# A hybrid DeltaNet and dilated-attention block: decay inputs moved into an attention unit, chain steps grouped, stores spread

## The chip, the cores and the metric

The kernel runs on one core of one Trainium2 chip, and the metric is its device time in microseconds. The engines are written as the profile writes them: PE is TensorE's matmul, PEld its weight load, DVE is VectorE, ACT is ScalarE, POOL is GpSimd and SP is SyncE, which here issues nearly all DMAs from its queue (SPq). "Clock" means the TensorE clock that the profile says was granted, 1.00 being the upper level.

## What is computed

One encoder layer on 512 tokens of width 1024, all in float32. A combined projection of the normed input feeds two branches, whose results are gated, merged, projected and added to the input; a convolved feed-forward network follows.

```python
h = RMSNorm(x); proj = h @ w_in
qkv_a, z_a, a_in, b_in, q_b, k_b, v_b, gate_a, gate_b = split(proj)
# branch A: bidirectional gated DeltaNet, 8 heads of 64, chunks of 64 tokens
q_a, k_a, v_a = silu(conv3(qkv_a));  q_a, k_a = l2norm(q_a), l2norm(k_a)
g = -exp(a_log) * softplus(a_in + dt_bias); beta = sigmoid(b_in)     # per direction and head
tmat = inverse(I + strict_lower((k*beta) @ k.T * decay))             # per chunk and head
...  # eight chunk steps that carry a state, both directions, summed, normed, * silu(z_a)
# branch B: attention, 3 groups of 8 heads, windows (128,1) (512,4) (2048,16), combined by softmax weights
x = x + (sigmoid(gate_a) * (o_a @ w_dn_out) + sigmoid(gate_b) * (o_b @ w_attn_out)) @ w_o
x = x + (silu(gate) * up) @ w_ffn_down      # gate, up = conv3(RMSNorm(x) @ w_ffn_up)
```

The decay inputs a_in and b_in are 32 columns of the projection in all: two directions by eight heads for each of the two.

## The kernel before

**Products.** Every large product is made of three matmuls on split numbers: mm3 (L321) multiplies high by high, high by low and low by high part, so PE's lines L322, L323 and L324 come in equal numbers. A dense tile is 128 output columns by 512 tokens: 8 blocks of the contraction by 3 matmuls, 24 matmuls 512 wide, in one dense PSUM tile (`dps`, four of them, PD). Chains use a second pool of four PSUM tiles (`gps`, PG).

**Weights.** Stream (L52) brings the weights in, in the order of use. SP loads a block into one of three staging tiles (`wst`, L67), ACT copies the high part (`whi`, L81), and POOL or DVE subtracts to get the low part (`wlo`, L83). Six pairs of parts are kept, three blocks ahead of use. SP's one queue also takes the chains' own loads and stores in the order in which the program issues them.

**The order of dense work** is written out by hand in SEQ (L39): K (four tiles), AB (the decay inputs: 32 columns, as 24 matmuls of 32 rows by 512 tokens), Q0 to Q3, U0, V0 to V3, Z0, U1, and so on to U11, then the last gates, YA, YB and WO. K, Q and V are the DeltaNet inputs, channels on partitions. A unit U is one attention group by two heads: 384 columns (q, k and v) as 96 matmuls 384 wide, tokens on partitions, in four dense PSUM tiles, one for each 128 tokens; att_dense (L642) takes all four at its start. Z and G tiles are the gates. Up to YA, chains run between the dense matmuls; after it comes a dense tail (YA, YB, WO, the feed-forward network).

**Chains.** All other work is in Python generators, and Driver (L121) places their steps while the program is built. It keeps a modelled time; each dense matmul group adds its cost, and after it due (L173) runs each chain step whose time has come. A chain's yield says how much later its next step may stand: LATE (1.5) after work whose result a PE step takes, LOAD (5.0) after a DMA, TRIP (8.0) after a round trip. The times are the planner's own and set only the order of instructions on each engine; at run time each engine takes its instructions in that order and waits on semaphores. room and need hold a step until a slot (T2: four [128, 512] work tiles; PG; PD) is free by the model.

**The chains that matter here.** After K, the row norm (L363 to L379) runs in line with the program and makes `rstd`. qkv_tile (L445) takes a Q, K or V tile from PSUM on DVE (L429), does the three-tap convolution (L432 on ACT, L434 and L435 on DVE), and the SiLU (L458, L459). decays (L488) transposes the AB rows on PE, does softplus and sigmoid arithmetic in 64-wide DVE and ACT steps (L505 to L525), and takes cumulative sums on PE (L531). k_tokens transposes K (L577). chain (L952) then forms the 64 by 64 systems and solves them in halves: eight stores of 32x32x32 pieces of `cx` go to DRAM in `dl`, in runs of 128 bytes (L987); one load brings them back as `lt` (L989); 31 solve steps of two DVE instructions each (L994, L997) follow; then a store, ten scattered loads back (L1014, L1017), block products, eight DeltaNet steps and post (L1288), which transposes the outputs (L1305) and splits them (`oa`, L1315, L1319) for YA. att_softmax (L728) takes each unit through scores, exps (Exp on ACT, L770), turn (four transposes per head and block of the probabilities, L782), and values (L798).

```python
def due(self, ahead=0.3):                                   # L173
    while True:
        d = [c for c in self.chains if c[1] <= self.now + ahead]
        if not d:
            return
        self.step(min(d, key=lambda c: c[1]))
...
for f in range(2):                                          # L982
    for a in range(2):
        for b in range(2):
            ...
            nc.sync.dma_start(du(dl)[f, a, b], cx[P, f].rearrange("p s h t -> p (s h) t")[:, :, b * 32:b * 32 + 32])     # L987
yield LOAD
nc.sync.dma_start(lt, dl)                                   # L989
```

## Time and profile before

| | |
|---|---|
| time, median of 3 runs | 1046.26 us (1045.7 to 1050.86) |
| time of the profiled execution | 1045.01 us |
| its span | 1043.2 us |
| mean granted clock | 0.982 |
| PE busy | 1001.0 us (96%), 6653 matmuls |
| PEld busy | 838.3 us (80%) |
| DVE busy | 676.1 us (65%) |
| ACT busy | 433.3 us (42%) |
| POOL busy | 252.8 us (24%) |

The times of the table are of one execution, the profiled one; what the span leaves out of its time is 1.8 us around the first and last instruction. A busy share is an average over stages with different limits, so the stage table (the first group of rows) is read first: it gives each engine's busy time in a stretch and how many instructions that is. The timeline then gives single waits: a bracket behind a row holds the idle time of the engine just before it and what ended that. A stretch of half clock shows only in the windows view, in the column after the busy times.

### The profile page before, as it was taken

The numbers are of one execution on the slowest core, as the hardware profiler recorded it, in microseconds if no ns is written. First come the engines' busy times: TensorE is split into PE (matmuls) and PEld (weight loads), VectorE is DVE, ScalarE is ACT, GpSimd is POOL, SyncE is SP. The second block draws the span as 40 slices with busy tenths as digits, with TensorE's granted clock in tenths as the row PEclk, the third lists the DMA queues.
The fourth block names the chain that finished last, engine by engine and source line by source line (L and its number), as shares of the span: only waits on it lengthen the run. The fifth ranks groups of instructions, "written<-read, shape, count | busy, mean of one in ns | idle before, by whom it ended". The sixth has DMA issues, their size and how long they took to land.

```text
span 1043.2 us, 17128 instructions
## 1 busy us (share of the span) xinstructions
PE 1001.0 (96%) x6653; PEld 838.3 (80%) x6653; DVE 676.1 (65%) x1139; ACT 433.3 (42%) x857; POOL 252.8 (24%) x229
## 2 busy tenths in 40 slices
PE   8989989987999989999999999899999999999998
PEld 7769788875998978988887878688888888888886
DVE  7594957756798746566867575577775326777621
ACT  6246545646554535324455133344433214344310
POOL 5334366623443532534532001200000000000000
PEclk9999989989999989999999999999999999999999
DMA  6223233462222491322365545313223222222331
GB/s 203 88 65 92 67 118 126 106 187 75 94 86 81 147 192 48 105 82 71 103 225 159 158 137 171 129 64 101 83 99 121 82 100 81 100 82 101 112 111 41
DMA packets 80289, 114.62 MB, mean 110 GB/s; under 512 B 32624, under 2 KB 45264, under 8 KB 79824
## 3 DMA queue, kind: packets, MB, share of 16 engines
q1 hardware_dynamic: 77328, 108.29, 33.8%
q10 hardware_dynamic: 2880, 5.24, 1.4%
q8 instruction: 52, 0.85, 0.3%
q14 instruction: 29, 0.24, 0.1%
HBM read 101.04 MB, written 12.47 MB: 109 GB/s over the span
## 4 chain that ended last, share of the span: by engine, by line
PE 67%; DVE 14%; issue 6%; ACT 5%; DMA 4%; POOL 2%; SPq 2%; POOLq 0%; ACTq 0%; DVEq 0%
PE dps L322 20%; PE dps L323 20%; PE dps L324 20%; DMA wst<-in_wa 3%; POOL wlo L83 2%; PE gps L747 1%; PE gps L798 1%; DVE wlo L83 1%; ACT sb L770 1%; DVE tmp L994 1%; ACT whi L81 1%; DVE ass L261 1%; PE gps L782 1%; DVE cy L434 1%; DVE ass L260 1%
## 5 line engine op out<-in xcount | busy, mean ns | idle before, releaser
L83 POOL TENSOR_TENSOR wlo<-wst,whi 128x384 fp32r<-128x384 f32 (+1 forms) x152 | 184.6, 1226 | 284.4 <-ACT whi L81 264.4
L81 ACT ACTIVATE whi<-wst 128x384 fp32r<-128x384 f32 (+2 forms) x259 | 174.4, 691 | 142.6 <-PE dps L323 70.7
L322 PE MATMUL dps<-h2h,whi 128*128 128x512 f32 x352 | 139.2, 395 | 0.0
L324 PE MATMUL dps<-h2h,wlo 128*128 128x512 f32 x352 | 139.1, 395 | 0.0
L323 PE MATMUL dps<-h2l,whi 128*128 128x512 f32 x352 | 139.0, 395 | 0.0
L83 DVE TENSOR_TENSOR wlo<-wst,whi 128x1024 fp32r<-128x1024 f32 (+2 forms) x107 | 117.6, 1106 | 20.9 <-ACT whi L81 20.8
L432 ACT ACTIVATE cy<-pre,vec 128x512 f32<-128x512 f32 x56 | 40.5, 724 | 142.1 <-DVE pre L429 142.0
L322 PE MATMUL dps<-whi,hr 128*128 128x384 f32 x256 | 92.3, 360 | 1.2 <-DVE v L672 0.6
L323 PE MATMUL dps<-wlo,hr 128*128 128x384 f32 x256 | 86.9, 339 | 0.0
L324 PE MATMUL dps<-whi,lr 128*128 128x384 f32 x256 | 86.9, 339 | 0.0
L323 PEld LDWEIGHTS dps<-h2l,whi 128*128 128x128 f32 x352 | 66.1, 188 | 16.0
L324 PEld LDWEIGHTS dps<-h2h,wlo 128*128 128x128 f32 x352 | 66.1, 188 | 16.0
L322 PEld LDWEIGHTS dps<-h2h,whi 128*128 128x128 f32 x352 | 66.1, 188 | 16.0
L434 DVE SCALAR_TENSOR_TENSOR cy<-pre,vec,cy 128x511 f32<-128x511 f32 x56 | 46.4, 828 | 36.3 <-ACT cy L432 36.3
L322 PE MATMUL dps<-ah,whi 128*128 128x512 f32 x176 | 69.8, 397 | 0.0
L323 PE MATMUL dps<-al__7594,whi 128*128 128x512 f32 x176 | 69.6, 396 | 0.0
L324 PE MATMUL dps<-ah,wlo 128*128 128x512 f32 x176 | 69.2, 393 | 0.0
L1430 DVE TENSOR_TENSOR x<-x,dps 128x512 f32<-128x512 f32 x16 | 11.0, 688 | 78.8 <-PE dps L324 78.8
L322 PE MATMUL dps<-hh,whi 128*128 128x512 f32 x128 | 53.4, 417 | 2.2 <-ACT hh L286 2.2
L770 ACT ACTIVATE sb<-sb,stat 128x128 f32<-128x128 f32 (+1 forms) x96 | 40.8, 426 | 33.9 <-DVE stat L759 33.8
L322 PE MATMUL dps<-hr,whi 128*128 128x512 f32 x120 | 50.0, 416 | 4.4 <-ACT v L677 4.4
L322 PE MATMUL dps<-whi,hh 128*128 128x384 f32 x128 | 46.7, 365 | 7.7 <-DVE z L1214 5.1
(298 smaller groups left out, 2116.2 us busy)
## 6 DMA issues: line engine op xcount, KB each, us to landing
wst<-in_wb SPq DMA_DIRECT2D x66, 512.0 KB, 3.2
wst<-in_wa SPq DMA_DIRECT2D x96, 256.0 KB, 2.7
wst<-in_wa SPq DMA_DIRECT2D x96, 192.0 KB, 2.4
xk<-in_xt SPq DMA_DIRECT2D x24, 256.0 KB, 3.6
dgt<-gt ACTq DMA_DIRECT2D x16, 256.0 KB, 2.8
alb<-daw SPq DMA_DIRECT2D x24, 128.0 KB, 3.0
dg<-dgd SPq DMA_DIRECT2D x16, 128.0 KB, 3.0
ga<-dgt SPq DMA_DIRECT2D x8, 256.0 KB, 5.6
```

Of the source, the lines that this page charges most:

```text
L81: self.drv.S(w).activation(hi[:, :w], st[:, :w], AF.Copy)
L83: eng(w).tensor_tensor(lo[:, :w], st[:, :w], hi[:, :w].bitcast(F32), ALU.subtract)
L260: V(n).tensor_mul(tmp, x, y)
L261: V(n).scalar_tensor_tensor(tmp, tmp, -0.5, y, op0=ALU.mult, op1=ALU.mult)
L322: nc.tensor.matmul(ps, wh, xh, start=first, stop=False)
L323: nc.tensor.matmul(ps, wh, xl, start=False, stop=False)
L324: nc.tensor.matmul(ps, wl, xh, start=False, stop=last)
L432: S(512).activation(y, pre, AF.Copy, scale=w[1])
L434: V(512).scalar_tensor_tensor(y[:, 1:], pre[:, :-1], w[0], y[:, 1:], op0=ALU.mult, op1=ALU.add)
L747: nc.tensor.matmul(pss[h][:, t], qT[H, x, i:i + 128], kT[H, y, i:i + w], start=(n == 0), stop=(n == 2))
L770: S(w, 1.15).activation(sbs[b, h][:, t], sbs[b, h][:, t], AF.Exp, bias=st[:, 0:1], accum_out=st[:, 1:2])
L1430: V(512).tensor_tensor(x1[:, d], x1[:, d], ps, ALU.add)
```

## The change

**The decay inputs** lose their own tile. SEQ no longer has AB; the 32 columns are appended to the first unit's weight blocks (WIDTH 416 for U0), so its 96 matmuls are 416 wide. They come out with tokens on partitions, so the four transposes in decays go, and ACT writes them out of the unit's PSUM in eight small copies. Q0 to Q2 now stand ahead of U0 and Q3 behind it; Q0 to Q2 use PG's PSUM tiles. The row norm becomes a chain of its own (rownorm) that runs under the first Q tile. A unit takes three dense PSUM tiles at its start and the fourth after its second block.

**Grouping.** A yield of "pe" (LATE, now 1.7) or "soon" (0.9) marks a chain whose next step is on PE. When due runs one such step, it also runs the others that are at least 0.6 (EARLY) past their last result. The turns of both heads of a block are now one step of eight transposes (turns), and the block products of both halves stand together.

**Buffers and DMAs.** T2 has six tiles for four, and qkv_tile takes them one by one; six pairs of weight parts become five. The eight scattered stores (`dl`), the scattered loads behind the solve and a few small stores each yield, so that other work can stand between them. LOAD goes from 5.0 to 4.5, the waits in combine to 3.0 (HOP).

```diff
-SEQ = ([("K", 0), ("AB", 0)] + [("Q", i) for i in range(4)] + [("U", 0)] + [("V", i) for i in range(4)]
+SEQ = ([("K", 0), ("Q", 0), ("Q", 1), ("Q", 2), ("U", 0), ("Q", 3)] + [("V", i) for i in range(4)]
...
-LOAD, TRIP, LATE = 5.0, 8.0, 1.5
+LOAD, HOP, TRIP, LATE, SOON, EARLY = 4.5, 3.0, 8.0, 1.7, 0.9, 0.6
...
-WIDTH = {"AB": 256, "U": 384}
+WIDTH = {"U": 384, ("U", 0): 416}
...
-            c[1] = max(self.end, self.now) + (r or 0.0)
+            end = max(self.end, self.now)
+            late = LATE if r == "pe" else SOON if r == "soon" else None
+            c[1], c[3] = (end + (r or 0.0), None) if late is None else (end + late, end + EARLY)
...
-            d = [c for c in self.chains if c[1] <= self.now + ahead]
+            d = [c for c in self.chains if c[1] <= self.now + ahead or batch and c[3] and c[3] <= self.now]
...
-            self.step(min(d, key=lambda c: c[1]))
+            c = min(d, key=lambda c: c[1])
+            batch = batch or c[3] is not None
+            self.step(c)
...
-    T2, PG, PD = Slots(4), Slots(4), Slots(4)
+    T2, PG, PD = Slots(6), Slots(4), Slots(4)
...
-    ws = Stream(drv, nc, wp, A["wa"], [WIDTH.get(n, 512) for n, _ in SEQ for _ in range(NBLK[n])], 3, 6, "a",
+    ws = Stream(drv, nc, wp, A["wa"], [WIDTH.get(x, WIDTH.get(x[0], 512)) for x in SEQ for _ in range(NBLK[x[0]])], 3, 5, "a",
...
-    psd = small_ps()
-    wh, wl = ws.block()
-    for k in range(KD):
-        mm3(psd[0:32], wh[:, k * 32:k * 32 + 32], wl[:, k * 32:k * 32 + 32], hh[k], hl[k], k == 0, k == KD - 1)
-    drv.dense(5.6)
...
+    drv.add(rownorm(), 0.8)
...
-        yield LATE
-        yield from drv.room(PG)
-        pt = small_ps()
-        for s in range(4):
-            nc.tensor.transpose(pt[:, s * 32:s * 32 + 32], ab[0:32, s * 128:s * 128 + 128], ident[0:32, 0:32])
-        pe(0.5)
+        while "ab" not in flags:
+            yield 0.3
...
-        pss = [dense_ps() for _ in range(4)]
+        first = g == 0 and p == 0
+        width = 416 if first else 384
+        drv.need(PD, 3)
+        pss = [dense_ps() for _ in range(3)]
...
+            if k == 1:
+                drv.need(PD)
+                pss.append(dense_ps())
+                mm(3, 0)
+                mm(3, 1)
...
+            if first:
+                for h in range(2):
+                    f, n = (1, 7 - 2 * i - h) if i > 1 else (0, 2 * i + h)
+                    S(32).activation(ab[HALF[f], n], ps[HALF[h], 384:416], AF.Copy, scale=r[HALF[h]])
...
-        def turn(b, h):
-            while not flags.get(("exp", u, b, h)):
+        def turns(b):
+            while ("exp", u, b, 0) not in flags or ("exp", u, b, 1) not in flags:
                 yield 0.3
...
+            yield "pe"
+            yield from drv.room(PG, 2)
+            for h in range(2):
...
                     nc.sync.dma_start(du(dl)[f, a, b], cx[P, f].rearrange("p s h t -> p (s h) t")[:, :, b * 32:b * 32 + 32])
+                    yield 1.2
...
                     nc.sync.dma_start(cxf[P, f, :, b * 32:b * 32 + 32], du(dx[1 if fwd else 0])[f, a, b])
+                    yield 0.6
```

The planner then sets all engines' instructions anew. At three places the two orders read as follows. First, DVE between the row norm and the first unit, before: the `pre0` rows are the arithmetic of decays, `pre` and `cy` the K tiles' convolutions.

```order
L505 TENSOR_TENSOR pre0_425<-gps_452,vec_74 64x32 x4
L509 SCALAR_TENSOR_TENSOR pre0_425<-pre0_425 128x64
L434 SCALAR_TENSOR_TENSOR cy_447<-pre_428,vec_74,cy_447 128x511
L435 SCALAR_TENSOR_TENSOR cy_447<-pre_428,vec_74,cy_447 128x511
L434 SCALAR_TENSOR_TENSOR cy_468<-pre_430,vec_74,cy_468 128x511
L435 SCALAR_TENSOR_TENSOR cy_468<-pre_430,vec_74,cy_468 128x511
L515 TENSOR_SCALAR pre0_425<-pre0_425 128x64
L516 RECIPROCAL pre0_425<-pre0_425 128x64
L517 TENSOR_TENSOR pre0_425<-pre0_425 128x64
```

And DVE from the row norm's end on, after the change:

```order
L386 COPY rstd_441<-gps_436 128x512
L438 TENSOR_TENSOR pre_443<-dps_80,rstd_441 128x512
L438 TENSOR_TENSOR pre_445<-dps_81,rstd_441 128x512
L438 TENSOR_TENSOR pre_447<-dps_82,rstd_441 128x512
L438 TENSOR_TENSOR pre_449<-dps_83,rstd_441 128x512
L443 SCALAR_TENSOR_TENSOR cy_457<-pre_443,vec_74,cy_457 128x511
L444 SCALAR_TENSOR_TENSOR cy_457<-pre_443,vec_74,cy_457 128x511
L443 SCALAR_TENSOR_TENSOR cy_464<-pre_445,vec_74,cy_464 128x511
L444 SCALAR_TENSOR_TENSOR cy_464<-pre_445,vec_74,cy_464 128x511
```

All four K tiles now leave PSUM in a row, and the decay arithmetic stands behind the first unit. Second, SP around the scattered stores, before; `wst` are weight blocks, `dl` the stores, `lt` their reload, `xk` blocks of the input.

```order
L826 DMA dog_419<-og_1891 128x512
L67 DMA wst_2120<-in_wa 128x384
L987 DMA dl_2140<-cx_402 32x32x32 x8
L67 DMA wst_2161<-in_wa 128x384
L67 DMA wst_2203<-in_wa 128x384
L989 DMA lt_2142<-dl_2140 128x2048
```

SP there after the change:

```order
L1003 DMA dl_2269<-cx_334 32x32x32 x2
L67 DMA wst_2312<-in_wa 128x512
L303 DMA xk_2321<-in_xt 128x512
L1003 DMA dl_2269<-cx_334 32x32x32
L67 DMA wst_2334<-in_wa 128x512
L67 DMA wst_2340<-in_wa 128x384
L303 DMA xk_2352<-in_xt 128x512
L1003 DMA dl_2269<-cx_334 32x32x32 x4
L67 DMA wst_2438<-in_wa 128x384
L67 DMA wst_2474<-in_wa 128x384
L1006 DMA lt_2271<-dl_2269 128x2048
```

Loads now stand between the stores, and the reload is still two weight blocks behind the last of them. Third, DVE at the first solve step, before; `sb` are attention scores, `xk` and `lr` the reordering of the input by residue classes.

```order
L757 SCALAR_TENSOR_TENSOR sb_2265<-acon_415,gps_2249 128x512
L759 TENSOR_REDUCE stat_2010<-sb_2265 128x2
L994 TENSOR_TENSOR tmp_2144<-lt_2142,xi_2143 128x62
L997 TENSOR_TENSOR xi_2143<-xi_2143,tmp_2144 128x2x31
L304 SCALAR_TENSOR_TENSOR xk_2008<-xk_2008,vec_74,rstd_389 128x512
L311 TENSOR_TENSOR lr_2294<-xk_2008,hr_2293 128x512
```

The same place after the change; `ass` is the norm of q and k of an attention unit, `qk` its scaling, `pt` a copy of transposed probabilities.

```order
L268 SCALAR_TENSOR_TENSOR ass_2448<-ass_2448 128x16
L1011 TENSOR_TENSOR tmp_2273<-lt_2271,xi_2272 128x62
L1014 TENSOR_TENSOR xi_2272<-xi_2272,tmp_2273 128x2x31
L713 TENSOR_TENSOR qk_2363<-qk_2363,ass_2448 128x1024
L804 COPY pt_2558<-gps_2557 128x512
L1011 TENSOR_TENSOR tmp_2273<-lt_2271,xi_2272 128x120
L1014 TENSOR_TENSOR xi_2272<-xi_2272,tmp_2273 128x2x30x2
```

Behind the first step there now stand a unit's scaling and a copy of probabilities, and no longer the reordering of the input.

## Rows read from the trace of the kernel before

**Rows 1.** Stages: start:end length, busy (count) PE PEld DVE ACT POOL, clock, DMA, GB/s

```profile
0.00:33.00 33.00, 29.51 (x123) 24.45 (x123) 19.09 (x18) 18.02 (x30) 17.00 (x16) 0.95 0.58 185
33.00:572.00 539.00, 507.93 (x4553) 442.50 (x4552) 382.62 (x767) 261.25 (x619) 226.19 (x207) 0.97 0.38 109
572.00:1044.00 472.00, 463.58 (x1980) 371.34 (x1979) 274.38 (x355) 154.08 (x209) 9.59 (x7) 1.00 0.31 105
```

**Rows 2.** Timeline, PE: start, duration, instruction, [idle before <-what ended it]

```profile
54.85 0.60 PE L531 MATMUL gps<-pre,con 128*128 128x32 f32 x4 [2.21 <-DVE pre L525]
...
71.85 0.44 PE L322 MATMUL dps<-whi,hh 128*128 128x384 f32 x1 [2.58 <-DVE pre L429]
...
133.91 0.69 PE L322 MATMUL dps<-whi,hh 128*128 128x384 f32 x1 [5.12 <-DVE z L1214]
...
220.49 0.93 PE L782 MATMUL gps<-con,sb 128*128 128x128 f32 x4 [1.34 <-ACT sb L770]
224.39 0.48 PE L782 MATMUL gps<-con,sb 128*128 128x128 f32 x1 [2.98 <-ACT sb L770]
...
240.23 0.50 PE L322 MATMUL dps<-hr,whi 128*128 128x512 f32 x1 [4.37 <-ACT v L677]
...
571.67 0.49 PE L322 MATMUL dps<-oa,whi 128*128 128x512 f32 x1 [2.17 <-ACT oa L1315]
```

**Rows 3.** Windows, PE alone: start:end length, busy (count), clock, DMA share, GB/s

```profile
56.70:60.10 3.40, 3.40 (x11) 0.50 0.01 2
...
131.80:138.60 6.80, 4.69 (x18) 0.50 0.34 109
223.90:230.70 6.80, 6.31 (x27) 0.50 0.31 94
```

**Rows 4.** Timeline, PE: first matmul of AB, what follows AB, and U0

```profile
33.38 0.40 PE L322 MATMUL gps<-hh,whi 128*32 128x512 f32 x1
...
38.92 0.60 PE L376 MATMUL gps<-con,rtok 128*128 128x128 f32 x4
...
87.10 0.34 PE L323 MATMUL dps<-wlo,hh 128*128 128x384 f32 x1
...
88.15 0.34 PE L323 MATMUL dps<-wlo,hh 128*128 128x384 f32 x1
```

**Rows 5.** Timeline, PE: one group of transposes, then a dense matmul

```profile
77.23 0.60 PE L577 MATMUL gps<-con,kq 128*128 128x128 f32 x4
77.59 0.42 PE L322 MATMUL dps<-whi,hh 128*128 128x384 f32 x1
```

**Rows 6.** Timeline of SP's DMA queue around the scattered stores

```profile
202.27 9.49 SPq L987 DMA_DIRECT2D dl<-cx  x8
211.86 2.36 SPq L67 DMA_DIRECT2D wst<-in_wa  x2
215.16 0.33 SPq L989 DMA_DIRECT2D lt<-dl  x1
```

**Rows 7.** Timeline, ACT and DVE behind those stores

```profile
215.80 0.53 ACT L81 ACTIVATE whi<-wst 128x384 fp32r<-128x384 f32 x1 [6.43 <-DMA wst<-in_wa]
...
221.03 0.26 DVE L994 TENSOR_TENSOR tmp<-lt,xi 128x62 f32<-128x62 f32 x1
```

**Rows 8.** Windows, columns of Rows 1: Q and U0; V; Z0 and U1

```profile
40.00:76.00 36.00, 31.20 (x145) 25.43 (x145) 33.26 (x66) 16.33 (x37) 11.84 (x10) 0.95 0.26 84
76.00:100.00 24.00, 24.00 (x142) 22.27 (x141) 10.38 (x19) 17.87 (x37) 11.24 (x11) 1.00 0.29 86
100.00:135.00 35.00, 29.88 (x178) 24.32 (x178) 32.45 (x68) 15.30 (x36) 12.86 (x16) 0.90 0.26 78
```

**Rows 9.** Timeline, DVE: two convolution steps of one K tile

```profile
44.75 0.75 DVE L435 SCALAR_TENSOR_TENSOR cy<-pre,vec,cy 128x511 f32<-128x511 f32 x1
45.42 1.79 DVE L434 SCALAR_TENSOR_TENSOR cy<-pre,vec,cy 128x511 f32<-128x511 f32 x1
```

**Rows 10.** Costliest groups: busy, mean ns | idle before, its main releaser

```profile
L81 ACT ACTIVATE whi<-wst 128x384 fp32r<-128x384 f32 (+2 forms) x259 | 174.4, 691 | 142.6 <-PE dps L323 70.7
```

More of the change, by code (lines that the diff above doesn't have):

```diff
@@ L158, in add @@
     def add(self, gen, delay=0.0):
-        c = [gen, self.now + delay, True]
+        c = [gen, self.now + delay, True, None]
         self.chains.append(c)
@@ L195, in finish, with room @@
         self.until(lambda: not c[2])
-    def room(self, slots, k=1):
-        while not slots.ready(k, self.now + 0.3):
+    def room(self, slots, k=1, spare=0):
+        while not slots.ready(k + spare, self.now + 0.3):
             yield 0.3
@@ L362, in hybrid, with rownorm @@
     rtmp = cp.tile([128, 2, 4], F32, name="rtmp")
-    rps = small_ps()
-    for i in range(4):
-        nc.tensor.matmul(rps[:, 2 * i:2 * i + 2], acc[:, i * 128:i * 128 + 128], ones[:, 0:2], start=True, stop=True)
-    pe(1.0)
-    V(8).tensor_copy(rtmp[:, 0], rps[:, 0:8:2])
-    newton(rtok[:, 0], rtmp[:, 0], rtmp[:, 1], 1.0 / D, EPS)
-    psd = small_ps()
-    wh, wl = ws.block()
-    for k in range(KD):
-        mm3(psd[0:32], wh[:, k * 32:k * 32 + 32], wl[:, k * 32:k * 32 + 32], hh[k], hl[k], k == 0, k == KD - 1)
-    drv.dense(5.6)
-    rps = small_ps()
-    for i in range(4):
-        nc.tensor.transpose(rps[:, i * 128:i * 128 + 128], rtok[:, 0, i:i + 1].to_broadcast([128, 128]), ident)
-    rstd = cp.tile([128, T], F32, name="rstd", tag="rstd")
-    pe(0.6)
-    V(512).tensor_copy(rstd, rps)
+    rstd_ = []
+    def rownorm():
+        yield from drv.room(PG)
+        rps = small_ps()
+        for i in range(4):
+            nc.tensor.matmul(rps[:, 2 * i:2 * i + 2], acc[:, i * 128:i * 128 + 128], ones[:, 0:2], start=True, stop=True)
+        pe(1.0)
+        V(8).tensor_copy(rtmp[:, 0], rps[:, 0:8:2])
+        drv.give(PG)
+        newton(rtok[:, 0], rtmp[:, 0], rtmp[:, 1], 1.0 / D, EPS)
+        yield "pe"
+        yield from drv.room(PG)
+        rps = small_ps()
+        for i in range(4):
+            nc.tensor.transpose(rps[:, i * 128:i * 128 + 128], rtok[:, 0, i:i + 1].to_broadcast([128, 128]), ident)
+        pe(0.6)
+        rstd_.append(cp.tile([128, T], F32, name="rstd", tag="rstd"))
+        V(512).tensor_copy(rstd_[0], rps)
+        drv.give(PG)
+    drv.add(rownorm(), 0.8)
     wqk = cp.tile([128, 1], F32, name="wqk")
@@ L445, in qkv_tile @@
     def qkv_tile(n, m, dst, ps, slots):
-        yield from drv.room(T2, 2)
+        while not rstd_:
+            yield 0.3
+        yield from drv.room(T2, 1, 2)
         tiles = []
-        for t in conv(ps, V_CW + 3 * m, rstd):
-            if not tiles:
+        for t in conv(ps, V_CW + 3 * m, rstd_[0]):
+            tiles.append(t)
+            if len(tiles) == 1:
                 drv.give(slots)
-            tiles.append(t)
-            yield
+                yield
+                yield from drv.room(T2)
+            else:
+                yield
         th, y = tiles[0], tiles[2]
@@ L653, in att_dense @@
             parts.append(ws.block())
-            for i in range(4 if k < KD - TAIL else 0):
+            for i in range(0 if k >= KD - TAIL else 4 if k > 1 else 3):
                 mm(i, k)
-            if k < KD - TAIL:
-                used.append(k)
+            if k == 1:
[3 more added lines that the diff above has]
+                mm(3, 1)
+            if 0 < k < KD - TAIL:
+                used.extend(range(2) if k == 1 else [k])
         qk = v = None
@@ L952, in chain @@
     def chain():
-        yield from decays()
+        dc = drv.add(decays())
         while done["K"] < 4:
             yield 0.3
-        yield LATE
+        yield "pe"
         yield from k_tokens()
-        while done["Q"] < 4:
+        while done["Q"] < 4 or dc[2]:
             yield 0.5
@@ L1039, in chain @@
                 drv.give(PG)
-                yield 0.5
+        for f, blk in enumerate(blks):
             for P0, P1, fwd in blk:
@@ L1043, in chain @@
                     G(512).memset(cxf[P1, f, :, 0:32], 0.0)
+        yield "pe"
+        for f, blk in enumerate(blks):
             for n0 in (0, 16):
@@ L1239, in gate @@
         drv.give(T2)
-    order = SEQ[SEQ.index(("U", 0)):SEQ.index(("YA", 0))]
+    order = SEQ[1:SEQ.index(("YA", 0))]
     classes = False
@@ L1246, in dense @@
             att_unit(i)
+        elif n == "Q" and i < 3:
+            drv.need(PG)
+            begin(qkv_tile("Q", i, kq[:, i, :, 1], h_dense(small_ps()), PG))
+            if i == 1:
+                nc.sync.dma_start(acon, A["acon"])
+        elif n == "Q":
+            begin(qkv_tile("Q", i, kq[:, i, :, 1], h_dense(), PD))
         elif n == "V":
```

138 lines of the change are left out of this document (62 added, 76 removed).

## The prediction

> **What bounds the kernel now.** I read the stage table first. It splits the run into the K projection (0 to 33 us), the stretch in which dense projections and attention and DeltaNet chains share TensorE (33 to 572), and the dense tail (572 to the end) [rows 1]. The reader is to see that TensorE is the bound in all three, that the tail has 463.58 us of work in 471 us at a clock of 1.00, and that the diff's core lies in the middle stretch. There TensorE is busy for 507.93 of 539.00 us and its mean granted clock is 0.97. So 31.1 us are idle, and the clock costs another 0.03 x 539 = 16 us. The change can win back at most these 47 us, plus what TensorE work it takes out.
>
> Next the timeline of TensorE: seven waits make 20.8 of the 31.1 us, and each row names who ended it [rows 2]. Five are on VectorE or ScalarE being late, two (220 and 224 us) on an Exp that ScalarE began late. Then the clock: stretches at 0.50, the lower of its levels (1.2 GHz), lie behind several of them [rows 3]. A stretch of 3.40 us at 0.50 does 1.7 us of full-clock work, so it costs 1.7, one of 6.80 us 3.4. Last, VectorE by stages: busy 33.26 of 36 us before 76 us, 10.38 of 24 after that, then 32.45 of 35 [rows 8]. It is overloaded in two bursts with a slack stretch between them.
>
> **The change part by part.** The sum is made against the profiled execution (1045.0 us, of which 1043.2 is the span); the median of the runs is 1.3 us above it.
>
> *1. Decay inputs inside the first attention unit.* The separate projection, 24 matmuls of 32 rows by 512 columns, runs from 33.38 to 38.92: 5.5 us [rows 4]. It goes. Instead the 96 matmuls of the first unit are 416 wide, not 384. Six 384-wide ones take 88.15 - 87.10 = 1.05, or 0.175 each; a 512-wide one takes 5.54/24 = 0.231; so 32 columns are about 0.014 us, and 96 of them 1.4 us. The four transposes of the old decay rows go too; a like group of four takes 77.59 - 77.23 = 0.36 us [rows 5]. Net -4.5 us, all on the path, since TensorE is the bound there. The row-norm arithmetic that the old matmuls covered now runs under the first Q tile (24 matmuls, 5.5 us as well): nothing.
>
> *2. Grouping of chain steps.* TensorE's order has 90 groups of small matmuls between dense ones, before 106. What does one entry and exit cost? Four transposes set in alone took 0.36 us until the next dense matmul [rows 5]. That is close to their own work, so a switch costs between nothing and some 0.1 us, and 16 fewer bring 0 to 1.6 us. I take 1.
>
> *3. The wait for the decays (54.85).* Before, 45 dense matmuls (10.4 us) stand between the decay transposes and the cumulative sums that wait 2.21 us for them, and a half-clock stretch follows [rows 2, 3]. Now 72 dense matmuls (Q3, V0, V1; 16.6 us) lie between the first unit's end and the cumulative sums. Gain 2.2 + 1.7 = 3.9 us, at worst 0.
>
> *4. The first unit's PSUM (71.85).* It waited 2.58 us for VectorE to evict Q tiles behind the decay arithmetic [rows 2]. That arithmetic leaves this burst: 23 instructions at no more than the stretch's mean of 33.26/66 = 0.50 us, so under 11.5 us; they are its short ones, I take 7. The wait goes. But the K transposes now stand 30 unit matmuls (6 us) after the unit's first, and need all four K tiles through VectorE, so up to 2 us may come back. I take -1.9.
>
> *5. The wait at Z0 (133.91).* 5.12 us and a 6.80 us half-clock stretch, 8.5 us in all [rows 2, 3]. One more dense tile (Q3, 5.5 us) now lies ahead of it, but the 7 us of decay arithmetic come too, part of which fits into what used to be the slack stretch. Bounds 0 and -8.5; I take -2.5, nearer to 0, since the burst's 32.45 of 35 us stay [rows 8].
>
> *6. Scattered stores.* Eight stores of 128-byte runs took SP's queue 9.49 us in a row [rows 6]. Weight loads queue behind them, and ScalarE, which splits those weights, sat idle 6.43 us for one [rows 7]. The Exp steps behind that split were late, hence the waits at 220.49 and 224.39 (4.3 us) and a 6.80 us half-clock stretch (3.4). Now weight and x loads stand between the stores, at most four stores in a row. That bounds a load's delay by half, under the 6.3 us that three blocks of a unit last (36 x 0.175), so the 7.7 us should go. What is late next: the DVE order now has the qk scaling and a probability copy behind the first solve step, which needs the reload of those stores, and TensorE's next group needs both. Before, that step began 221.03 - 215.16 = 5.9 us after the reload's issue [rows 6, 7], so between 0 and 5.9 us come back. I take 1.7: net -6.0. The 4.37 us at 240.23 (ScalarE's evictions behind the reordering copies) stay.
>
> By the Trainium skill ("DMA: Bandwidth & Descriptors", Issuing engines are not separate DMA queues) the time of issuing a DMA is usually small beside the DMA itself. Here eight issues held the queue 9.49 us, so the row speaks otherwise; by the page, spacing them out would bring nothing, this term would be 0 and the sum 6 us higher.
>
> *7. The end of the chains (571.67).* TensorE waits 2.17 us for the last DeltaNet output. Its last transposes now stand 3 dense matmuls before that point, before 9. So the wait grows by 6 x 0.231 = 1.4 us.
>
> *8. The rest.* Six T2 buffers for four, weight parts in five for six. ScalarE already waits for TensorE before splits (70.7 us in all) [rows 10], so one buffer less makes that wait longer, hidden by the 6.3 us lead; were it not, a unit block (2.1 us) each time. The 10.3 us of smaller waits stay: 0, plus or minus 5.
>
> Sum: -4.5 - 1 - 3.9 - 1.9 - 2.5 - 6.0 + 1.4 = -18.4. That gives 1026.6 on the profiled execution, and about 1028 on the median's scale.
>
> **The rivals.**
> *A. VectorE stays the bound (waits move, they don't go).* For it: 32.45 of 35 us busy at Z0, with more arithmetic brought in [rows 8]. Then 7 us of decay work against 2.55 us of slack give 4.5 us more wait at Z0 in place of the 2.5 gained, and the K transposes take all of the 1.9: 1028 + 4.5 + 2.5 + 1.9 = 1037. A neighbour in the rows makes it worse: two equal convolution steps took 0.75 and 1.79 us [rows 9], the slower one beside GpSimd's splits. The Trainium skill ("SBUF — State Buffer", Who interferes with whom) says why: a VectorE operation with two SBUF inputs and a GpSimd one block each other for a whole instruction; the trace agrees, with 1.04 us here. Against it: the slack stretch takes in part of the work.
>
> *B. Slower.* Grouped transposes are issued sooner after their inputs, and a waiting matmul holds all dense work behind it. There are 16 such groups of probability transposes. If each waits as at 220.49 (1.34 us) and half of them bring a half-clock stretch (1.7), that is 16 x 1.34 + 8 x 1.7 = 35 us: 1063. It decides from about 1.5 us a group, where the 18.4 gained are used up and 5 more. Against it: by the order, most inputs keep a dozen or more dense matmuls of distance, as before.
>
> *C. The change doesn't do what it says.* The stores stay a jam (SP's work is the same) and only terms 1 to 3 hold, less 1.4: 1046.3 - 8.0 = 1038.
>
> *D. Nearly all waits go.* Terms 3 to 6 at their best (3.9 + 2.6 + 8.5 + 7.7) and half of the 10.3: 1046.3 - 5.5 - 27.9 = 1013.
>
> **How the numbers follow.** Forecast 0.57, own range 1018 to 1036; A 0.15, C 0.10, D 0.10, B 0.08. The 80% range reaches to D's and over A's and C's: 1008 to 1042. What this kernel's measurement can tell from no change is about 0.5%, 5.2 us, so "same" is 1041 to 1051.5. Faster: the forecast and D, and A and C for most of their spread, 0.82; same 0.10, the ends of A and C; slower 0.08.
>
> **What would show it.** Right: between K and Q0 no matmul of 32 rows; the cumulative sums start without a wait; between 200 and 230 us no ScalarE idle on a weight load; a wait of some 3 to 5 us left at Z0 and of 3 to 4 before the first output projection; mean clock of the middle stretch 0.98. Wrong: waits of over 1.5 us in front of the paired transposes all along (B), a wait at Z0 over 8 us (A), ScalarE still idle on weight loads near the scattered stores (C), or a new wait in the K loop or the tail, which I take as unchanged.

## The result

The changed kernel takes 1029.44 us (median of 4 runs, 1028.98 to 1031.27), the one before 1046.07 (4 runs, 1045.70 to 1050.86): a ratio of 0.983, 95% interval 0.980 to 0.987, so 16.6 us less. The forecast was 1028. The profiled execution took 1029.56 us (its span is 1027.8), where 1026.6 were forecast on that scale. The time came out as forecast; several of the terms it was summed from did not, as the sections below show.

The stage table of after answers to [rows 1], with the same columns (the middle stretch now ends at 556.40):

```profile
0.00:33.00 33.00, 29.35 (x121) 24.04 (x122) 18.96 (x18) 18.43 (x30) 16.87 (x17) 0.95 0.62 191
33.00:556.40 523.40, 499.81 (x4526) 439.94 (x4524) 390.37 (x762) 263.55 (x626) 227.68 (x206) 0.98 0.39 113
556.40:1028.00 471.60, 463.59 (x1980) 371.31 (x1979) 274.35 (x355) 154.18 (x209) 9.58 (x7) 1.00 0.33 105
```

All of the gain lies in the middle stretch: 539.0 us became 523.4, the tail kept its 472. TensorE's busy time there fell by 8.1 us, its idle time from 31.1 to 23.6. The timeline of TensorE after the change, as [rows 2], shows what waits are left:

```profile
72.12 0.50 PE L328 MATMUL dps<-hh,whi 128*128 128x512 f32 x1 [1.53 <-ACT pre L688]
...
91.13 0.63 PE L529 MATMUL gps<-pre,con 128*128 128x32 f32 x4 [2.01 <-DVE pre L523]
...
158.30 1.06 PE L724 MATMUL gps<-con,qk 128*128 128x128 f32 x4 [2.92 <-DVE qk L713]
...
221.79 0.50 PE L328 MATMUL dps<-hr,whi 128*128 128x512 f32 x1 [1.64 <-ACT v L684]
...
368.05 0.21 PE L1049 MATMUL gps<-cx 32*32 32x32 f32 x1 [1.81 <-ACT og L820]
...
384.61 0.26 PE L1072 MATMUL gps<-qt,aux 32*32 32x32 f32 x1 [1.84 <-issue]
...
507.54 0.65 PE L1122 MATMUL gps<-r,cx 64*64 64x64 f32 x15 [1.53 <-DVE r L1114]
...
556.07 0.51 PE L328 MATMUL dps<-oa,whi 128*128 128x512 f32 x1 [2.30 <-ACT oa L1334]
```

The 5.12 us at the second unit (they stand at its tenth matmul, the first that needs its fourth PSUM tile) and the two waits on an Exp, 1.34 and 2.98 us, are gone without a successor. The cumulative sums still wait for the decays, 2.01 where it was 2.21, and there are new waits: 1.53 behind the first unit, 2.92 on the scaling of q and k, 1.53 in a DeltaNet step. The last row, the first output projection, had waited 2.17. The half-clock stretches, as [rows 3] with the same columns, moved too:

```profile
103.80:110.60 6.80, 6.80 (x23) 0.50 0.26 74
158.40:161.80 3.40, 3.40 (x14) 0.50 0.09 25
370.00:376.80 6.80, 6.80 (x117) 0.50 0.03 7
383.70:390.50 6.80, 5.89 (x59) 0.50 0.01 4
```

Where the time went is best read at points that both kernels pass with the same dense work done: the start of the first matmul of a unit, read from the timelines. The table gives for each kernel how much earlier (-) or later that is than in the kernel named in its row, in us, from the profiled executions. "End of U1" is the first dense matmul behind U1, "gates" the first gate tile behind U11. The points fix the dense work, not the chains' work between it: a kernel that is ahead may still owe chain steps.

| kernel, against | U1 | end of U1 | U2 | U3 | U4 | U8 | U9 | gates | span |
|---|---|---|---|---|---|---|---|---|---|
| after, before | -7.0 | -14.3 | -13.0 | -11.6 | -20.9 | -21.1 | -21.4 | -19.1 | -15.4 |
| e1, before | -0.9 | +0.5 | +3.3 | +2.2 | -1.5 | -4.8 | -2.1 | -2.1 | -3.0 |
| e2, before | +0.1 | 0.0 | 0.0 | 0.0 | -4.9 | -4.9 | -6.1 | -6.0 | -7.9 |
| e3, before | -0.4 | -6.9 | -6.9 | -6.8 | -14.4 | -14.7 | -6.8 | -8.6 | -7.4 |
| e9, before | +2.6 | -1.2 | 0.0 | +2.3 | +0.5 | +15.6 | +11.7 | +13.2 | +10.8 |
| e4, after | +1.6 | +2.4 | +2.4 | +4.2 | +11.3 | +9.1 | +6.7 | +13.8 | +11.8 |
| e5, after | +1.6 | +1.6 | +1.6 | +1.6 | +12.8 | +10.7 | +16.1 | +17.8 | +15.5 |
| e7, after | +2.4 | +7.1 | +7.1 | +7.1 | +7.0 | +5.9 | +9.4 | +11.5 | +9.6 |
| e10, after | +2.6 | +2.5 | +1.2 | +0.2 | +5.0 | +13.3 | +18.7 | +19.5 | +15.8 |
| e11, after | -0.3 | -0.4 | -0.3 | -0.4 | -0.4 | -0.3 | -12.0 | -6.3 | -7.2 |
| e12, after | +2.7 | +2.8 | +2.8 | +2.7 | +2.7 | +3.0 | -8.0 | -10.5 | +16.9 |

In the first row the gain is made at two places, around the second unit (-14.3 by its end) and in and behind the fourth, U3 (from -11.6 to -20.9). Between the two 2.7 us are lost, behind the second hardly anything changes until U9, and from there 6 us are lost towards the end.

A word on precision: one program's runs differ by some microseconds (24 runs of the kernel before on one chip lay between 1040.65 and 1052.24, median 1045.46). The medians and intervals carry the verdicts; the profiles show the places. The kernel before had medians of 1045.3 to 1046.8 in the sets of runs beside the experiments, so 1 or 2 us between two variants are not told apart.

### The profile page after: what moved, and what is told of

It is laid out like the page before. It is cut to its first block, busy times and chain, and to the rows that moved or that the text cites. A ratio compares the mean times of both kernels' runs of the same rounds, so it can differ in the third digit from the quotient of the medians.

```text
span 1027.8 us, 17036 instructions
## 1 busy us (share of the span) xinstructions
PE 992.8 (97%) x6625; PEld 835.3 (81%) x6625; DVE 683.7 (67%) x1134; ACT 436.1 (42%) x864; POOL 254.1 (25%) x229
## 4 chain that ended last, share of the span: by engine, by line
PE 43%; DVE 4%; DMA 2%; ACT 2%; issue 1%; POOL 0%; SPq 0%; POOLq 0%; ACTq 0%; DVEq 0%
PE dps L328 14%; PE dps L330 14%; PE dps L329 14%; DVE wlo L83 1%; DMA wst<-in_wb 1%; DMA xo<-dob 1%; DVE ga L1373 1%; DMA ga<-dgt 1%; DMA wst<-in_wa 1%; ACT mh L1374 0%; DVE gb L1371 0%; PE gps L762 0%; ACT sq L1397 0%; PE gps L1122 0%; ACT whi L81 0%
## 5 line engine op out<-in xcount | busy, mean ns | idle before, releaser
L83 POOL TENSOR_TENSOR wlo<-wst,whi 128x384 fp32r<-128x384 f32 (+2 forms) x152 | 186.4, 1236 | 267.9 <-ACT whi L81 247.2
L81 ACT ACTIVATE whi<-wst 128x384 fp32r<-128x384 f32 (+3 forms) x258 | 175.6, 694 | 174.4 <-PE dps L329 78.7
L83 DVE TENSOR_TENSOR wlo<-wst,whi 128x1024 fp32r<-128x1024 f32 (+1 forms) x106 | 116.4, 1106 | 21.5 <-ACT whi L81 21.3
L330 PEld LDWEIGHTS dps<-h2h,wlo 128*128 128x128 f32 x352 | 66.1, 188 | 16.1
L443 DVE SCALAR_TENSOR_TENSOR cy<-pre,vec,cy 128x511 f32<-128x511 f32 x56 | 43.6, 779 | 36.3 <-ACT cy L441 36.3
L328 PE MATMUL dps<-hh,whi 128*128 128x512 f32 x112 | 46.9, 419 | 4.5 <-ACT hh L292 2.6
L328 PEld LDWEIGHTS dps<-whi,hr 128*128 128x128 f32 x256 | 48.3, 189 | 3.0 <-issue 1.4
```

Of the source, the lines that this page charges most:

```text
L81: self.drv.S(w).activation(hi[:, :w], st[:, :w], AF.Copy)
L83: eng(w).tensor_tensor(lo[:, :w], st[:, :w], hi[:, :w].bitcast(F32), ALU.subtract)
L328: nc.tensor.matmul(ps, wh, xh, start=first, stop=False)
L330: nc.tensor.matmul(ps, wl, xh, start=False, stop=last)
L443: V(512).scalar_tensor_tensor(y[:, 1:], pre[:, :-1], w[0], y[:, 1:], op0=ALU.mult, op1=ALU.add)
```

## The experiments

Two theories stood against each other for the first place. One says that a unit's PSUM handling removed the wait; the other, the prediction's, that VectorE now gets its work done in time, since one more dense tile (Q3) lies ahead and part of the decay arithmetic falls into the slack stretch; the expectations call it the lighter burst. For the second place, the spread stores against SP's total work. E1 to E3 put one part each into the kernel before.

**E1, the decay inputs alone.** AB goes from SEQ, the first unit gets its 32 columns, decays waits for the unit. Ahead of that unit the plan also asks for four free PSUM tiles, which its order needs there.

```diff
-SEQ = ([("K", 0), ("AB", 0)] + [("Q", i) for i in range(4)] + [("U", 0)] + [("V", i) for i in range(4)]
+SEQ = ([("K", 0)] + [("Q", i) for i in range(4)] + [("U", 0)] + [("V", i) for i in range(4)]
...
-WIDTH = {"AB": 256, "U": 384}
+WIDTH = {"U": 384, ("U", 0): 416}
```

> The kernel before with one part of the change: the decay inputs come out of the first unit's columns, no AB tile, decays a chain of its own that waits for the unit. If the removed TensorE work is the gain, 4 to 6 us less than before: 1040 to 1042, and the wait of 5.12 us ahead of the second unit stays, to within 2 us. If the lighter VectorE burst is what removed that wait (rival), its 5.12 us and its half-clock stretch go too: 1032 to 1035.

Measured: 1041.84 us against 1045.46 (ratio 0.996, 0.994 to 0.999), 3.6 us less. TensorE's timeline in this kernel:

```profile
66.89 0.46 PE L322 MATMUL dps<-whi,hh 128*128 128x416 f32 x1 [3.87 <-DVE pre L430]
...
133.14 0.69 PE L322 MATMUL dps<-whi,hh 128*128 128x384 f32 x1 [5.29 <-DVE z L1208]
```

The 3.6 us are somewhat less than the 4.5 that the prediction summed for this part, but the interval (1.1 to 6.8 us) holds both. The unit comes earlier and waits 3.87 us for its PSUM where it waited 2.58. And the 5.12 us at the second unit are still there, 5.29, although the decay arithmetic has left the earlier burst. So moving the decays alone does not remove that wait. E1 leaves Q3 ahead of the first unit, so it does not test the further dense tile.

**E2, the spread stores alone.**

```diff
                     nc.sync.dma_start(du(dl)[f, a, b], cx[P, f].rearrange("p s h t -> p (s h) t")[:, :, b * 32:b * 32 + 32])
+                    yield 1.2
```

> The kernel before with only the eight scattered stores spread (one yield of 1.2 behind each). If the jam on SP's queue made the two waits of 1.34 and 2.98 us and the half-clock stretch behind them, these go and the time falls by 5 to 8 us: 1038 to 1041. If SP's total work or the later reload holds the chains anyway (rival), 1044 to 1048, with ScalarE still idle for more than 4 us on a weight load near 210 us.

Measured: 1039.70 us (ratio 0.992, 0.990 to 0.995), 5.8 us less. The table shows it at one place: nothing before U3, -4.9 at U4, and in this profile 3 us more by the end. The waits of 1.34 and 2.98 us are gone, the 4.37 us one behind the unit grew, since ScalarE's evictions still come late:

```profile
234.29 0.80 PE L322 MATMUL dps<-hr,whi 128*128 128x512 f32 x1 [6.32 <-ACT v L677]
```

**E3, the units' PSUM alone.** Three tiles at the start, asked for in the plan and given back, the fourth after the second block.

```diff
-        pss = [dense_ps() for _ in range(4)]
+        drv.need(PD, 3)
+        pss = [dense_ps() for _ in range(3)]
...
+            if k == 1:
+                drv.need(PD)
+                pss.append(dense_ps())
+                mm(3, 0)
+                mm(3, 1)
```

> The kernel before with only the units' PSUM handled as in the change: three tiles at the start, asked for and given back in the plan, the fourth after the second block. If that is what removed the wait ahead of the second unit, its 5.12 us and its 6.8 us of half clock go: 7 to 9 us less, 1037 to 1039. If the wait went because VectorE's burst became lighter (rival), the wait stays over 3 us or comes back within 20 us of it, and the time is 1043 to 1047.

Measured: 1038.06 us (ratio 0.993, 0.990 to 0.996), 7.4 us less. The wait is gone; by the table its place gives 6.5 us (from -0.4 to -6.9). TensorE's timeline first, the start of the unit and the fourth tile's first matmul behind a group of attention values; then VectorE's, the eviction of Z0:

```profile
126.58 0.69 PE L322 MATMUL dps<-whi,hh 128*128 128x384 f32 x1
...
131.88 0.44 PE L322 MATMUL dps<-whi,hh 128*128 128x384 f32 x1
```

```profile
130.82 0.68 DVE L1221 TENSOR_TENSOR z<-dps,rstd 128x512 f32<-128x512 f32 x1
```

VectorE empties Z0's tile from 130.82 to 131.50, and it is wanted only after 18 matmuls of the other three tiles, at 131.88. In the kernel before it was wanted after nine; the last of them on TensorE's timeline is

```profile
128.45 0.34 PE L324 MATMUL dps<-whi,lh 128*128 128x384 f32 x1
```

and the tile came at 133.91 [rows 2]. So the plan, which now knows of the tile, has it emptied 2.4 us earlier, and the unit wants it over 3 us later. In the kernel before, the PSUM handling alone is enough at the first place. It also gains 7.6 us at the second (from -6.8 at U3 to -14.4 at U4), with the stores still in a row, where E2 gained 4.9: the second place does not belong to the stores alone. The kernel had reached -14.7 at U8 and lost 7.9 of it between U8 and U9, where the block products are; E11 comes back to that place.

**E4, the change without the PSUM handling.** The diff of E3 taken out of the changed kernel.

> The changed kernel with the units' PSUM handled as before: four tiles at the start, not asked for in the plan. If that handling is worth the wait ahead of the second unit, such a wait of 3 to 5 us and a half-clock stretch come back: 1035 to 1039. If the lighter burst or the six buffers are what removed it (rival), 1028 to 1032.

Measured: 1042.17 us (ratio 0.996, 0.994 to 0.999), 12.7 us more than the change, beyond the 6 to 10 that were expected, and not in the place expected: at U1 no long wait comes back (+1.6, +2.4 by its end). It is at later units and their neighbours that TensorE now waits:

```profile
204.59 0.69 PE L328 MATMUL dps<-whi,hh 128*128 128x384 f32 x1 [2.25 <-DVE gt L1239]
...
231.01 0.50 PE L328 MATMUL dps<-hr,whi 128*128 128x512 f32 x1 [3.71 <-ACT v L678]
...
404.35 0.86 PE L1115 MATMUL gps<-vs,cx 64*64 64x64 f32 x22 [3.70 <-POOL vs L1092]
```

So at U1 itself the handling (E3) or the rest of the change (here) is enough alone, while the later units lose without it (+2.4 at U2, +11.3 at U4). VectorE's timeline at Z0's tile, first in the change and then here, shows why U1 can do without:

```profile
120.12 0.69 DVE L1226 TENSOR_TENSOR z<-dps,rstd 128x512 f32<-128x512 f32 x1 [0.46 <-PE dps L330]
```

```profile
122.16 0.68 DVE L1219 TENSOR_TENSOR z<-dps,rstd 128x512 f32<-128x512 f32 x1
```

In the change VectorE stood idle for 0.46 us until Z0's last matmul was done, and emptied the tile at once. It has no arrears there any more, with the old handling hardly any, where the kernel before got to this tile only shortly before 133.91 [rows 2]. That is the prediction's theory, and in the change it holds too. Its own cause, Q3's new place, was tried in no run by itself.

**E5, the change without the spread stores.**

```diff
-                    yield 1.2
```

> The changed kernel with the eight scattered stores in a row again. On the kernel before, spreading alone took 5.7 us off. If that part adds to the others, 5 to 7 us come back: 1034 to 1037, with waits and a half-clock stretch on TensorE in the fourth unit. If the other parts already gave the chains enough lead (rival), 1028 to 1031.

Measured: 1041.69 us (ratio 0.996, 0.994 to 0.999), 12.3 us more, twice what was expected (5 to 7). SP's queue, ScalarE and TensorE in this kernel, from the timelines of the three:

```profile
208.19 8.35 SPq L1003 DMA_DIRECT2D dl<-cx  x8
```

```profile
225.05 0.63 ACT L81 ACTIVATE whi<-wst 128x512 fp32r<-128x512 f32 x1 [3.89 <-DMA wst<-in_wa]
```

```profile
228.87 0.79 PE L328 MATMUL dps<-hr,whi 128*128 128x512 f32 x1 [7.12 <-ACT v L684]
```

The jam is the one of before: 8.35 us of stores, a weight block late, ScalarE idle, TensorE waiting 7.12 us, and half clock from 224.80 to 235.04 and again from 245.28 to 248.69. The table puts 11.2 of the 15.5 us of this profile between U3 and U4. In the changed kernel the stores look like this:

```profile
206.59 0.42 SPq L1003 DMA_DIRECT2D dl<-cx  x1
...
211.14 1.03 SPq L1003 DMA_DIRECT2D dl<-cx  x2
...
214.78 0.43 SPq L1003 DMA_DIRECT2D dl<-cx  x1
...
221.50 3.59 SPq L1003 DMA_DIRECT2D dl<-cx  x4
...
228.76 0.33 SPq L1006 DMA_DIRECT2D lt<-dl  x1
```

One or two of them take about 0.5 us each, four in a row 0.9 each, eight in a row 1.04 (1.19 before [rows 6]); together 5.47 us, not 8.35.

**E6, no grouping by the planner.** EARLY 99 for 0.6; turns and block products stay together as written.

> The changed kernel where the planner doesn't run TensorE steps of several chains together (EARLY 99; the turns of both heads and the block products stay together as written). If a switch costs up to 0.1 us, as the prediction has it, 0.5 to 2 us more: 1030 to 1032. If grouping sets steps too early and so makes waits (rival B of the prediction), it is faster: 1024 to 1028.

Measured: 1031.49 us (ratio 0.985, 0.981 to 0.990; the change has 0.983, 0.980 to 0.987). 2.1 us more in the medians, with intervals that overlap: unclear, of the sign and size forecast, and not rival B's.

**E7, four T2 buffers** for six, the rest of the change kept.

> The changed kernel with four T2 buffers instead of six. If the buffers cost and bring nothing, as the prediction has it, 1028 to 1031. If they are what lets VectorE empty PSUM ahead of the units (rival), waits of over 3 us come back ahead of the first two units and it is 5 us or more slower: 1034 to 1040.

Measured: 1038.60 us (ratio 0.992, 0.988 to 0.996), 9.2 us more. By the table 4.7 of it stand at U1, where a chain's wait and a wait on Z0's tile are back, with a half-clock stretch (they are smaller than the 3 us that were expected):

```profile
129.42 1.09 PE L814 MATMUL gps<-pt,v 128*64 128x128 f32 x16 [1.67 <-DVE pt L804]
...
131.35 0.69 PE L328 MATMUL dps<-whi,hh 128*128 128x384 f32 x1 [0.83 <-DVE z L1226]
```

VectorE empties Z0's tile 10 us later than in the change:

```profile
130.61 0.68 DVE L1226 TENSOR_TENSOR z<-dps,rstd 128x512 f32<-128x512 f32 x1
```

The prediction had costed the buffers at nothing.

**E8, a longer distance for the DeltaNet steps.** SOON 1.7 for 0.9.

> The changed kernel where the DeltaNet steps keep the distance of the other TensorE steps (SOON 1.7 instead of 0.9). Three waits of 1.03, 1.25 and 1.53 us on VectorE stand ahead of their matmuls after the change. If the short distance makes them, they go and the time falls by 2 to 4 us, to 1025 to 1027. If the steps then end later and the wait of 2.30 us for the last output grows by as much (rival), 1028 to 1031.

Measured: 1029.11 us (ratio 0.983, 0.979 to 0.988): no difference. The rival's time came, not its mechanism, which wanted the last wait to grow. In the profile the waits of 1.03, 1.25 and 1.53 us gave way to two others of 2.15 and 3.74 at the same steps, and the last one, 2.30, went.

**E9, three parts together in the kernel before:** the edits of E2 and E3 and six T2 buffers with five weight parts, without the AB part and the grouping. The change also has qkv_tile take its T2 tiles one by one; E9 does not.

> The kernel before with three parts of the change together: the units' PSUM handling, the spread stores, and six T2 buffers with five weight parts. The AB tile, the old turns and the ungrouped steps stay. If these three hold nearly all of the gain, 1030 to 1034. If the AB tile and the grouping are needed for it (rival; the PSUM handling alone lost 13 us again at the block products), 1036 to 1042.

Measured: 1052.83 us (ratio 1.006, 1.004 to 1.008): slower than before, by 6 us, where either of two of its parts alone gained 6 to 7. Neither theory had that. TensorE's timeline:

```profile
57.87 0.97 PE L531 MATMUL gps<-pre,con 128*128 128x32 f32 x4 [3.53 <-DVE pre L525]
...
250.78 0.48 PE L805 MATMUL gps<-pt,v 128*64 128x128 f32 x2 [4.93 <-DVE pt L794]
...
368.05 0.79 PE L322 MATMUL dps<-hr,whi 128*128 128x512 f32 x1 [5.52 <-DVE v L678]
```

With six buffers three K tiles' convolutions instead of two are let in ahead of the decay arithmetic, and the cumulative sums wait 3.53 us, not 2.21; of the gain at U3 (-8.3 in that unit) 6.5 are given back by U4; and 15 us go between U4 and U8, the largest wait there being 5.52 us on the unit's values. What in the change keeps these from happening was not taken apart.

**E10, three waits aimed at.** The decay inputs leave PSUM by VectorE, the scaling of q and k gets 3.7 us of distance (which also takes its next step out of the grouping), SOON 1.7.

```diff
-                    S(32).activation(ab[HALF[f], n], ps[HALF[h], 384:416], AF.Copy, scale=r[HALF[h]])
+                    V(32).tensor_scalar(ab[HALF[f], n], ps[HALF[h], 384:416], r[HALF[h]], None, op0=ALU.mult)
...
                               .to_broadcast([128, 4, 4, 64]), ALU.mult)
-        yield "pe"
+        yield 3.7
```

> The changed kernel with three waits aimed at: the decay inputs copied out of the first unit's PSUM by VectorE instead of ScalarE, 3.7 instead of 1.7 behind the scaling of q and k, and SOON 1.7. If the waits of 1.53, 2.01, 2.92, 0.79 and 1.16 us come from these places, 5 to 8 us with their half-clock stretches go: 1021 to 1025. If they move to the next step as waits did in the other runs (rival), 1027 to 1032.

Measured: 1042.59 us (ratio 0.996, 0.994 to 0.999), 13.2 us slower than the change and outside both ranges. The three waits on the scaling of q and k (2.92, 0.79 and 1.16) went, but others came:

```profile
72.97 0.47 PE L328 MATMUL dps<-hh,whi 128*128 128x512 f32 x1 [1.63 <-DVE pre L688]
...
159.24 0.45 PE L328 MATMUL dps<-whi,hh 128*128 128x384 f32 x1 [2.64 <-DVE z L1226]
```

The wait behind the first unit is the same whichever engine copies the decay inputs (1.53 and 1.63), so the choice of engine isn't its cause; whether the copies themselves are was not tried. The wait at 158 us goes from the scaling to the fourth PSUM tile of the same unit, and later ones of 3.14 us on an Exp (225.07) and 2.99 us on transposed probabilities (245.89) are new.

**E11, block products apart.** The changed kernel with a yield of 0.5 behind each of their groups, so that dense work stands between them.

> The changed kernel with the block products taken apart again, so that dense work can stand between their groups. After the change two half-clock stretches of 6.8 us lie there, before it two of 3.4. If the long run of small matmuls makes them, 2 to 4 us less: 1025 to 1028. If dense work between the groups only adds switches and waits (rival), 1029 to 1033.

Measured: 1027.19 us (5 runs, 1022.36 to 1028.57; ratio 0.982, 0.977 to 0.986), 2.3 us less than the change in the medians, with overlapping intervals. Its profiled execution was the fastest of its runs. The windows view from U8's start on, all engines, columns as in [rows 1], of the changed kernel and then of E11:

```profile
344.00:393.40 49.40, 45.33 (x747) 41.13 (x746) 21.83 (x35) 20.05 (x47) 16.47 (x15) 0.86 0.51 106
```

```profile
343.80:381.40 37.60, 34.80 (x459) 31.12 (x457) 18.57 (x36) 17.17 (x42) 12.60 (x12) 1.00 0.68 137
381.40:414.00 32.60, 29.83 (x514) 27.81 (x515) 16.32 (x37) 13.43 (x36) 12.42 (x12) 0.95 0.33 95
```

From U8 to U9 the clock is 1.00 instead of 0.86, and the unit and its gate take 37.4 us instead of 49.1. Part of it is moved work (459 matmuls for 747), which U9 then has: it takes 32.65 us for 27.85. Its five runs have a mean granted clock of 0.987 to 0.992, the change's four 0.983 to 0.987. So taking the long run of 32x32 matmuls apart took the two half-clock stretches away. The waits of 1.81 and 1.84 us inside the run went with it, so which of the two let the clock fall is not shown; and products that stand apart are no guarantee: in E3 they do, and the clock is at half for 13.7 us from 357.31 on, around a wait of 3.39 us that ends at 358.61. This kernel has the lowest median here, by less than its interval.

**E12, E11 with SOON 1.7.**

> The changed kernel with the block products taken apart and SOON 1.7 together. Apart they gave 1027.2 and 1029.1 us against 1029.4. If the waits of the DeltaNet steps are then rarer and nothing else moves, 1024 to 1027. If every new order of the steps brings its own waits, as the three parts together did on the kernel before (rival), anything from 1027 to 1036.

Measured: 1046.13 us (12 runs; ratio 1.001, 0.999 to 1.003): all of the gain gone, and outside both ranges. The two yields still do to the clock what they did in E11: from 360 to 400 us the granted clock is 0.79 in E8, which lacks them, and 0.96 here. By the table this kernel was 10.5 us ahead of the change at the gates and then lost 27; but it was ahead in dense work only, with 673 small matmuls left to do before the first output projection where the change has 345 (on the timelines). There the last DeltaNet steps stand with little dense work between them, and a ScalarE that waits for a reload holds the weights behind it. TensorE's timeline, then ScalarE's:

```profile
518.99 1.32 PE L1124 MATMUL gps<-r,cx 64*64 64x64 f32 x23 [3.68 <-DVE r L1116]
...
556.34 0.79 PE L328 MATMUL dps<-hr,whi 128*128 128x512 f32 x1 [5.74 <-ACT whi L81]
```

```profile
553.65 0.63 ACT L257 ACTIVATE ob<-xo 128x512 fp32r<-128x512 f32 x1 [11.73 <-DMA xo<-dob]
```

The split of a reloaded attention output (L257) stands ahead of the weight splits on ScalarE and waited 11.73 us for its load.

## Why the prediction was right, and where it was not

The number holds in part by luck, because errors of its terms cancel. By the table, terms 1, 3, 4 and 5 (-12.8 in sum) gave -14.3 by the end of U1, term 6 (-6.0) gave -9.3 at U3; against that, 2.7 us were lost between the two places and 6.0 behind U9, where only +1.4 was forecast. In its order:

- *1, decay inputs (-4.5).* The removed work is as sized: between its first matmul and that of the next tile the unit takes 20.2 us without its wait (21.75 - 1.53), before 18.9 (21.52 - 2.58), so it grew by 1.3 (1.4 forecast). That all of it lies on the path is not shown: alone the part brought 3.6 us in E1, whose interval holds 4.5, and the unit that now comes earlier waited 1.3 us longer for VectorE there.
- *2, grouping (-1).* E6 has 2.1 us of the same sign, unclear.
- *3, the wait for the decays (-3.9).* This step failed: 2.01 us are left of 2.21. The half-clock stretch of 3.40 us behind it [rows 3] went, worth 1.7, but at 103.80 one of 6.80 stands where before one of 3.4 stood, which takes as much back. The prediction counted the dense matmuls between and took the arithmetic to run at once. An Exp of the decays ends on ScalarE at 81.22, and VectorE goes on with them (L513) only at 86.69. VectorE's timeline after shows what stands in its way, the norm of the first unit's q and k (`ass`); ScalarE's and GpSimd's timelines are below it:

```profile
80.78 1.18 DVE L266 TENSOR_TENSOR ass<-ass 128x16 f32<-128x16 f32 x1
81.99 1.22 DVE L267 SCALAR_TENSOR_TENSOR ass<-ass 128x16 f32<-128x16 f32 x1
83.25 1.22 DVE L268 SCALAR_TENSOR_TENSOR ass<-ass 128x16 f32<-128x16 f32 x1
84.50 0.17 DVE L266 TENSOR_TENSOR ass<-ass 128x16 f32<-128x16 f32 x1
...
86.69 0.18 DVE L513 TENSOR_SCALAR pre<-pre 128x64 f32<-128x64 f32 x1
```

```profile
80.98 0.24 ACT L510 ACTIVATE pre<-pre 128x64 f32<-128x64 f32 x1
```

```profile
80.63 3.80 POOL L83 TENSOR_TENSOR wlo<-wst,whi 128x512 fp32r<-128x512 f32 x3 [1.18 <-ACT whi L81]
```

  Instructions of 16 elements take 1.2 us there instead of 0.17 for as long as GpSimd runs its splits (80.63 to 84.43). The three shown cost 3.1 us more than the same kind takes alone, more than the wait of 2.01. That is read from the trace; it was not tried apart.
- *4, the first unit's PSUM (-1.9).* The wait of 2.58 went, and one of 1.53 stands behind the unit: -1.1, inside what was allowed for.
- *5, the wait at Z0 (-2.5).* The term that was most off: 8.5 us came, its outer bound. The reason given, VectorE in time, holds in the change (0.46 us idle ahead of Z0's tile), but the prediction took the burst to stay. It left out two parts that were in the diff: the three tiles at a unit's start, which in E3 remove this wait with the old burst in place, and the six buffers, which it had put at nothing and without which a part comes back at the same unit (E7). The decay arithmetic's new place alone does nothing here (E1).
- *6, scattered stores (-6.0).* Right in mechanism, and in size when alone: 5.8 us in E2. In the change the place gave 9.3: the 4.37 us that were to stay became 1.64, and the half-clock stretch behind them went. In E2 that wait grew to 6.32, so its shrinking is not the stores' doing; E3, whose PSUM handling alone gained 7.6 us there, points to what the sum left out. What was said to be late next did not wait: the first solve step came 237.38 - 228.76 = 8.6 us after its reload's issue, later than the 5.9 of before, but no matmul waited for it there. VectorE's timeline has the step as

```profile
237.38 0.26 DVE L1011 TENSOR_TENSOR tmp<-lt,xi 128x62 f32<-128x62 f32 x1
```

  By the Trainium skill ("DMA: Bandwidth & Descriptors", Issuing engines are not separate DMA queues) issue time is usually small beside the transfer. For one store that is not contradicted: 1.19 us of issue, 5.4 from issue to landing (median, DMA view of before). But eight in a row held the queue 9.49 us [rows 6], and spacing them was worth 5.8, so the reading that would have made this term 0 failed.
- *7, the end of the chains (+1.4).* 2.30 for 2.17: +0.1.
- *8, the rest (0, plus or minus 5).* The block products now run at half clock for two stretches of 6.8 us, before for two of 3.4: +3.4. From U8 to U9 that is made up, not by waits (TensorE is idle for 4.0 us of 49.4 before and 4.1 of 49.1 after), but by 64 fewer matmuls (746 for 810), which stand elsewhere. From U9 to the span's end 6 us are lost, the DeltaNet steps' waits (1.03, 1.25 and 1.53 us) among them. The grouping was weighed as switches and not as what it does to the clock.

The rivals: A fell, since VectorE had no arrears left at Z0. C's condition did not come, nor D's. B's price was not paid as described, though its mechanism, a step set too close behind its input, fits the waits of 2.92, 0.79 and 1.16 us on the scaling of q and k, which went when E10 gave that step more distance. Of the signs named, the cumulative sums without a wait, the 3 to 5 us left at Z0 and the 3 to 4 before the first output projection (2.30) did not come; no ScalarE idle on a weight load between 200 and 230 us and the clock of 0.98 did.

What stays open is why the parts don't add. Taking away one of three parts from the change costs 12.7, 12.3 and 9.2 us, 34 in sum, where the whole gained 16.6; nearly the same three alone in the old kernel cost 6 together (E9). Each edit makes the planner order everything behind it anew, and E9, E10 and E12 show the new waits, but which property of an order makes it good was not found. Nor was Q3's new place tried by itself.

## What to carry to other kernels

Before a wait is put down to a busy engine, look at who asked for the resource and when: a tile that is wanted nine matmuls later may need no faster eviction. Where an order is made by a planner, an edit's price holds only for the order it was measured in, so measure a part both alone and taken out of the whole, and distrust sums. Here, small scattered stores did better between the loads of a shared queue than in a row.

## What the runs showed of the hardware

- TensorE was at half clock (granted 0.50, the lower level of 1.2 GHz) while it was busy all the time: 6.80 of 6.80 us from 370.00 and from 103.80 on. The first stretch begins 5 us into the run of 32x32 matmuls (365.04 to 372.71, with the wait of 1.81 us in it), and its second part is dense matmuls; the second begins 2.5 us into 32 matmuls two columns wide that no wait of TensorE interrupts. TensorE's windows and timeline after:

```profile
370.00:372.70 2.70, 2.70 (x107) 0.50 0.08 18
```

```profile
101.35 4.80 PE L604 MATMUL gps<-con,pre 128*128 128x2 f32 x32
```

  With dense matmuls between the groups of 32x32 matmuls the clock stayed at 1.00 (E11, 343.80 to 381.40); in E3, where they stand apart too, it did not (0.50 from 357.31 on).
- VectorE instructions of 16 elements with two inputs in SBUF took 1.18 to 1.22 us beside GpSimd's two-input splits (80.78 to 84.47) and 0.17 without. By the Trainium skill ("SBUF — State Buffer", Who interferes with whom) a VectorE instruction with two SBUF inputs contends with a GpSimd instruction that reads SBUF, and the shared ports are locked exclusively; the trace agrees, and the loss does not depend on how small the VectorE instruction is (1.05 us for 16 elements, 1.04 for 511 [rows 9]). It is not confined to two inputs: two one-input steps of such a norm took 0.96 and 0.93 us beside splits (232.89 and 233.88), where 0.17 is usual.
- A scattered store of 128-byte runs held the queue 0.4 to 0.5 us alone or as one of two, and 1.0 to 1.2 us as one of eight.
